# The combine of two expert outputs on one core: 16 rows of zeroes, 4096 bytes long in place of 512, taken from the last load room

## The chip, the cores and the metric

The kernel runs on one core of one Trainium2 chip. The metric is device time in microseconds, the median of several executions. VectorE (DVE) and ScalarE (ACT) compute; SyncE (SP) and ACT issue DMAs, each on a queue of its own. In the profile q1 is SP's queue and q10 is ACT's. Both are served by the same 16 DMA engines of the core.

## The reference

```python
def reference(expert_outputs, combine_weights):     # (16, 1024, 2, 512), (16, 1024, 2), float32
    weights = combine_weights[..., np.newaxis]
    return np.sum(expert_outputs * weights, axis=2).astype(np.float32)   # (16, 1024, 512)
```

For each of 16 x 1024 = 16384 tokens two rows of 512 floats are multiplied by one weight each and added. The inputs are 67 MB of rows and 0.13 MB of weights, the output is 33.5 MB. There is little arithmetic to a byte.

## The kernel before, in words

The tokens are laid over 128 partitions, 128 tokens to a partition. Of these the first 115 (`main`) are consecutive tokens of the partition; the last 13 come from the end of the array. One token is 4096 bytes of input (two rows) in a partition.

The tokens of a partition are cut into ten tiles of 13 or 12 (`TILES`). The large SBUF tile `et` holds 51 tokens for each partition and is divided into four rooms (`ROOM`, with their starts in `SITE`); tile g goes to room g modulo 4. So four tiles can be in SBUF at a time, and the load of tile g + 4 has to wait until the store of tile g has read its result out of the room.

The work is ordered by hand. SP issues the loads (L76) one after the other: five at the start, of which the first brings only 2 tokens and the second the other 11 of tile 0, then tiles 1, 2 and 3 (the fifth load fills the last room). Each later load follows the store that frees its room. For most tiles (`WHOLE`) VectorE multiplies the whole room by the weights in place (L88) and adds the two halves (L97); the sum lies in the first half of the room, and the store (L130) writes it out from there. Tile 8 (`MIXED`) is shared with ACT (L92, L94, L96), and the last tile is done token by token by ACT (L102) and VectorE (L103). The stores go out on ACT's queue, except the last two, which SP issues: tiles 7 and 8 in one, and tile 9.

What the change touches stands ahead of the loop. VectorE sets a small tile `zt` to zero (L108). ACT then issues, in this order on its queue: a DMA that writes these zeroes into 16 places of the output (L111), the weights of the first 115 tokens (L79, called in L112), and the weights of the last 13 in two halves (L114). After that ACT loads its table and does a warm-up activation (L115). The 16 places are the starts of 16 equal stretches of 920 output rows. Eight partitions' output makes one such stretch. The zeroes are overwritten later by store 0, the store of tile 0, which therefore has to wait for them. The first product of VectorE (L88) needs the weights and the first two loads.

Of the kernel before, what the change touches and what calls it, by code (L numbers as in the profile page):

```python
# [1 line left out]

# [4 lines left out]


@with_exitstack
def kernel(  # L10
    ctx: ExitStack,
    tc: tile.TileContext,
    expert_outputs: bass.AP,
    combine_weights: bass.AP,
    out: bass.AP,
):

    nc = tc.nc
    b, s, k, h = expert_outputs.shape
    assert k == 2
    n = b * s
    P = nc.NUM_PARTITIONS
    per = n // P
    assert per * P == n

    ROOM = [13, 13, 12, 13]
    ROOMS = len(ROOM)  # L30
    SITE = [sum(ROOM[:i]) for i in range(ROOMS)]
    TILES = [13, 13, 12, 13, 13, 13, 12, 13, 13, 13]
    FIRST = [2, 11, 13, 12, 13]
    STORES = [[0], [1], [2], [3], [4], [5], [6], [7, 8], [9]]
    WHOLE = [0, 1, 2, 3, 4, 5, 6, 7]
    MIXED = [8]
    ALONE = 3
    FREE = {9: 0}
    LAST = 13
    assert all(c <= ROOM[g % ROOMS] for g, c in enumerate(TILES))  # L40
    assert sum(TILES) == per and [g for st in STORES for g in st] == list(range(len(TILES)))
    main = per - LAST
    starts = [sum(TILES[:g]) for g in range(len(TILES))]

    def rows(x):

        first = x[0 : P * main, :].rearrange("(p t) f -> p t f", p=P)
        second = x[P * main : n, :].rearrange("(p t) f -> p t f", p=P)
        return lambda t, c: first[:, t : t + c, :] if t < main else second[:, t - main : t - main + c, :]

    flat = out.rearrange("b s h -> (b s) h")
    eo = rows(expert_outputs.rearrange("b s k h -> (b s) (k h)"))
    cw = rows(combine_weights.rearrange("b s k -> (b s) k"))
    o = rows(flat)

    dt = mybir.dt.float32
    mult = mybir.AluOpType.mult
    add = mybir.AluOpType.add
    copy = mybir.ActivationFunctionType.Copy

    pool = ctx.enter_context(tc.tile_pool(name="all", bufs=1))
    et = pool.tile([P, sum(ROOM), k * h], dt)
    halves = et.rearrange("p j (k h) -> p (j k) h", k=k)
    wt = pool.tile([P, per * k], dt)
    wk = wt.rearrange("p (t k) -> p t k", k=k)
    zt = pool.tile([16, 128], dt)
    warm = pool.tile([P, 1], dt)

    def place(t):
        g = max(g for g in range(len(TILES)) if starts[g] <= t)  # L70
        return SITE[g % ROOMS] + t - starts[g]

    def load(t, c, **kw):
        at = place(t)
        assert place(t + c - 1) == at + c - 1
        nc.sync.dma_start(out=et[:, at : at + c], in_=eo(t, c), **kw)  # L76

    def weights(q, t, c):
        q.dma_start(out=wk[:, t : t + c, :], in_=cw(t, c))  # L79

    def combine(g, base):
        at, c, t0 = SITE[g % ROOMS], TILES[g], starts[g]
        if g in WHOLE or g in MIXED:
            room = halves[:, k * at : k * (at + c), :]
            x0, x1 = et[:, at : at + c, 0:h], et[:, at : at + c, h : 2 * h]
            if g in WHOLE:
                wb = wt[:, k * t0 : k * (t0 + c)].unsqueeze(2).to_broadcast([P, k * c, h])
                nc.vector.tensor_tensor(out=room, in0=room, in1=wb, op=mult)  # L88
            else:
                for i in range(ALONE, c):  # L90
                    x = et[:, at + i, 0:h]
                    nc.scalar.activation(out=x, in_=x, func=copy, scale=wt[:, k * (t0 + i) : k * (t0 + i) + 1])  # L92
                w1 = wk[:, t0 : t0 + c, 1:2].to_broadcast([P, c, h])
                nc.vector.tensor_tensor(out=x1, in0=x1, in1=w1, op=mult)  # L94
                w0 = wk[:, t0 : t0 + ALONE, 0:1].to_broadcast([P, ALONE, h])
                nc.vector.tensor_tensor(out=x0[:, 0:ALONE], in0=x0[:, 0:ALONE], in1=w0, op=mult)  # L96
            nc.vector.tensor_tensor(out=halves[:, base : base + c, :], in0=x0, in1=x1, op=add)  # L97
            return
        for i in range(c):
            t = k * (t0 + i)  # L100
            x0, x1 = halves[:, k * (at + i), :], halves[:, k * (at + i) + 1, :]
            nc.scalar.activation(out=x0, in_=x0, func=copy, scale=wt[:, t : t + 1])  # L102
            nc.vector.scalar_tensor_tensor(  # L103
                out=halves[:, base + i, :], in0=x1, scalar=wt[:, t + 1 : t + 2], in1=x0, op0=mult, op1=add
            )

    with tc.manual_schedule():
        nc.vector.memset(zt, 0.0)  # L108

        ahead = flat[0 : P * main, :].rearrange("(q t) h -> q (t h)", q=16)  # L110
        nc.scalar.dma_start(out=ahead[:, 0:128], in_=zt)  # L111
        weights(nc.scalar, 0, main)  # L112
        for half in (slice(0, P // 2), slice(P // 2, P)):
            nc.scalar.dma_start(out=wk[half, main:per, :], in_=cw(main, per - main)[half])  # L114
        nc.scalar.activation(out=warm, in_=nc.const_aps.tensor(1.0, (P, 1), dt), func=copy)  # L115

        t = 0
        for i, c in enumerate(FIRST):
            load(t, c, **({"max_dma_last_dim": k * h * 4} if i == 0 else {}))
            t += c  # L120
        assert t == sum(TILES[:ROOMS])
        for j, st in enumerate(STORES):
            room = FREE.get(st[0], st[0] % ROOMS)
            base, c = SITE[room] * k, 0
            for g in st:
                combine(g, base + c)
                c += TILES[g]
            assert c <= k * ROOM[room]
            q = nc.sync if j in (7, 8) else nc.scalar
            q.dma_start(out=o(starts[st[0]], c), in_=halves[:, base : base + c, :])  # L130
            for g in st:
                if g + ROOMS < len(TILES):
                    load(starts[g + ROOMS], TILES[g + ROOMS])


# [1 line left out]
_INS = ['expert_outputs', 'combine_weights']  # L137
_OUTS = [((16, 1024, 512), 'float32')]


# [23 lines left out]
```

## Time and profile before

| what | value |
|---|---|
| median of 3 runs | 238.86 us (238.84 to 238.99) |
| span of the profiled execution, first to last instruction | 237.1 us |
| VectorE busy | 190.0 us, 80% of the span |
| ACT busy | 15.8 us, 7% |
| moved by DMA | 100.80 MB, mean 425 GB/s over the span |
| zeroes: memset, DMA | 165 ns; 8 KB, 3.9 us from issue to landing |
| weights of 115 tokens | 115 KB, 18.2 us from issue to landing |

The profiled execution's time is known by its span; the runs' median is 1.8 us above it, which is what lies around the first and the last instruction. "Busy" leaves out the instructions that only issue DMAs, wait or branch. The DMA row of the page shows the mean share of the 16 DMA engines' time in each of 40 slices, in tenths. The groups of instructions give the line, the engine, the tiles written and read, the shape, and how long one takes. In the chain of waits each row is a start, a duration and what was then being waited for.

### The profile page before, as it was taken

The numbers are of one execution on the slowest core, as the hardware profiler recorded it, in microseconds if no ns is written. First come the engines' busy times: TensorE is split into PE (matmuls) and PEld (weight loads), VectorE is DVE, ScalarE is ACT, GpSimd is POOL, SyncE is SP. The second block draws the span as 40 slices with busy tenths as digits, with TensorE's granted clock in tenths as the row PEclk, the third lists the DMA queues.
The fourth block names the chain that finished last, engine by engine and source line by source line (L and its number), as shares of the span: only waits on it lengthen the run. The fifth ranks groups of instructions, "written<-read, shape, count | busy, mean of one in ns | idle before, by whom it ended". The sixth has DMA issues, their size and how long they took to land.

```text
span 237.1 us, 154 instructions
## 1 busy us (share of the span) xinstructions
DVE 190.0 (80%) x33; ACT 15.8 (7%) x25; POOL 0.2 (0%) x4
## 2 busy tenths in 40 slices
DVE  0006999999999999999999998998499969919400
ACT  2000000000000000000000000000000055019200
POOL 0000000000000000000000000000000000000000
DMA  8999999989999999999899999999899999899996
GB/s 300 388 481 434 432 421 398 470 348 485 449 431 458 431 440 390 486 420 420 359 492 409 409 509 392 431 503 431 359 431 503 420 397 483 381 431 431 431 431 287
DMA packets 3344, 100.80 MB, mean 425 GB/s; under 512 B 512, under 2 KB 656, under 8 KB 912
## 3 DMA queue, kind: packets, MB, share of 16 engines
q1 hardware_dynamic: 2000, 77.33, 75.9%
q10 hardware_dynamic: 1344, 23.47, 23.0%
HBM read 67.24 MB, written 33.56 MB: 425 GB/s over the span
## 4 chain that ended last, share of the span: by engine, by line
DVE 55%; DMA 36%; issue 1%; ACT 0%; DVEq 0%; ACTq 0%; SPq 0%
DVE et L88 35%; DVE et L97 17%; DMA out_dram<-et 17%; DMA et<-in_expert_outputs_dram 12%; DMA wt<-in_combine_weights_dram 8%; DVE et L103 3%; ACT et L102 0%; DVEq L159 0%; ACTq L111 0%; DVE zt L108 0%; DVEq L88 0%; SPq L76 0%; ACTq L102 0%
## 5 line engine op out<-in xcount | busy, mean ns | idle before, releaser
L88 DVE TENSOR_TENSOR et<-et,wt 128x13312 f32<-128x13312 f32 (+1 forms) x8 | 110.0, 13754 | 23.8 <-DMA wt<-in_combine_weights_dram 18.7
L97 DVE TENSOR_TENSOR et<-et 128x6656 f32<-128x6656 f32 (+1 forms) x9 | 62.8, 6973 | 0.4
L92 ACT ACTIVATE et<-et,wt 128x512 f32<-128x512 f32 x10 | 6.2, 708 | 188.0 <-DMA et<-in_expert_outputs_dram 188.0
L103 DVE SCALAR_TENSOR_TENSOR et<-et,wt 128x512 f32<-128x512 f32 x13 | 8.7, 747 | 5.0 <-ACT et L102 5.0
L102 ACT ACTIVATE et<-et,wt 128x512 f32<-128x512 f32 x13 | 8.1, 707 | 14.0 <-DMA et<-in_expert_outputs_dram 14.0
L94 DVE TENSOR_TENSOR et<-et,wt 128x6656 f32<-128x6656 f32 x1 | 7.1, 7093 | 2.3 <-DMA et<-in_expert_outputs_dram 2.3
L96 DVE TENSOR_TENSOR et<-et,wt 128x1536 f32<-128x1536 f32 x1 | 1.8, 1751 | 0.0
L115 ACT ACT_TABLE_LOAD x1 | 1.3, 1283 | 3.1 <-issue 3.1
L108 DVE MEMSET zt<- 16x128 f32 x1 | 0.2, 165 | 0.8 <-PEq L148 0.8
L115 ACT ACTIVATE warm<-const-float32-1.0 128x1 f32<-128x1 f32 x1 | 0.2, 203 | 0.0
L148 POOL MEMSET const-bfloat16-1.0<- 128x1 bf16 x1 | 0.1, 102 | 0.0
L148 POOL MEMSET const-uint8-127<- 128x1 uint8 x1 | 0.1, 101 | 0.0
L148 POOL MEMSET const-float32-0.0<- 128x1 f32 x1 | 0.1, 99 | 0.2 <-issue 0.2
L148 POOL MEMSET const-float32-1.0<- 128x1 f32 x1 | 0.1, 98 | 0.0
## 6 DMA issues: line engine op xcount, KB each, us to landing
et<-in_expert_outputs_dram SPq DMA_DIRECT2D x7, 6656.0 KB, 32.2
out_dram<-et ACTq DMA_DIRECT2D x5, 3328.0 KB, 34.7
et<-in_expert_outputs_dram SPq DMA_DIRECT2D x2, 6144.0 KB, 41.1
out_dram<-et SPq DMA_DIRECT2D x1, 6656.0 KB, 19.9
out_dram<-et ACTq DMA_DIRECT2D x2, 3072.0 KB, 37.2
et<-in_expert_outputs_dram SPq DMA_DIRECT2D x1, 5632.0 KB, 18.2
out_dram<-et SPq DMA_DIRECT2D x1, 3328.0 KB, 14.0
et<-in_expert_outputs_dram SPq DMA_DIRECT2D x1, 1024.0 KB, 5.0
```

Of the source, the lines that this page charges most:

```text
L88: nc.vector.tensor_tensor(out=room, in0=room, in1=wb, op=mult)
L92: nc.scalar.activation(out=x, in_=x, func=copy, scale=wt[:, k * (t0 + i) : k * (t0 + i) + 1])
L94: nc.vector.tensor_tensor(out=x1, in0=x1, in1=w1, op=mult)
L96: nc.vector.tensor_tensor(out=x0[:, 0:ALONE], in0=x0[:, 0:ALONE], in1=w0, op=mult)
L97: nc.vector.tensor_tensor(out=halves[:, base : base + c, :], in0=x0, in1=x1, op=add)
L102: nc.scalar.activation(out=x0, in_=x0, func=copy, scale=wt[:, t : t + 1])
L103: nc.vector.scalar_tensor_tensor(out=halves[:, base + i, :], in0=x1, scalar=wt[:, t + 1 : t + 2], in1=x0, op0=mult, op1=add)
L108: nc.vector.memset(zt, 0.0)
L115: nc.scalar.activation(out=warm, in_=nc.const_aps.tensor(1.0, (P, 1), dt), func=copy)
L148: nc = _bacc.Bacc("TRN2", target_bir_lowering=False, num_devices=1)
```

## The change

The tile `zt` of 16 x 128 floats is no longer allocated. In its place a view of `et` is taken: partitions 0 to 15, the first token of the last room, all 1024 floats of it. It is set to zero by the same memset, now of 16 x 1024 elements. The DMA writes 1024 floats (`k * h`), two output rows, at each of the 16 places, in place of 128 floats, a quarter of a row. The room is filled by the fifth load afterwards, so this load has to come after the zeroes have been read.

```diff
     wk = wt.rearrange("p (t k) -> p t k", k=k)
-    zt = pool.tile([16, 128], dt)
     warm = pool.tile([P, 1], dt)
...
     with tc.manual_schedule():
+        zt = et[0:16, SITE[ROOMS - 1], :]
         nc.vector.memset(zt, 0.0)
 
         ahead = flat[0 : P * main, :].rearrange("(q t) h -> q (t h)", q=16)
-        nc.scalar.dma_start(out=ahead[:, 0:128], in_=zt)
+        nc.scalar.dma_start(out=ahead[:, 0 : k * h], in_=zt)
         weights(nc.scalar, 0, main)
```

## The prediction

> **What bounds the kernel now.** I read the page first: its slices, the DMA queues and the share that the packets took.
>
> ```profile
> span 237.1 us, 154 instructions
> ...
> DVE 190.0 (80%) x33; ACT 15.8 (7%) x25; POOL 0.2 (0%) x4
> ...
> DMA  8999999989999999999899999999899999899996
> ...
> q1 hardware_dynamic: 2000, 77.33, 75.9%
> q10 hardware_dynamic: 1344, 23.47, 23.0%
> ```
>
> The two queues (q1 is issued by SP, q10 by ACT) fill 75.9% + 23.0% = 98.9% of what 16 DMA engines could do in the span. VectorE has 80%. Next, the busy time by stretches; the last two columns are the DMA share and GB/s.
>
> ```profile
> 1.80:5.00 3.20, 0.00 (x0) 1.49 (x2) 0.00 (x0) 1.00 0.99 315
> 8.30:10.00 1.70, 0.00 (x0) 0.00 (x0) 0.00 (x0) 1.00 1.00 433
> 41.60:49.50 7.90, 7.90 (x1) 0.00 (x0) 0.00 (x0) 1.00 0.99 406
> 1.80:236.00 234.20, 189.85 (x32) 15.79 (x25) 0.00 (x0) 1.00 1.00 430
> ```
>
> From 1.8 us to 236 us the DMA engines have no gap (share 1.00, 430 GB/s). So the time is the bytes over this rate, plus 1.8 us ahead of the first packet and 1.1 us behind the last. Two stretches run below the undisturbed 433 GB/s: the first 3.2 us (315) and the 7.9 us in which the first store starts (406).
>
> Then the chain of waits, which reads differently at first sight:
>
> ```profile
> 0.81 0.17 DVE zt L108
> ...
> 1.01 0.39 ACTq L111
> ...
> 1.43 18.21 DMA wt<-in_combine_weights_dram
> ...
> 19.73 14.04 DVE et L88
> ...
> 144.62 39.25 DMA out_dram<-et
> ...
> 183.92 28.80 DMA et<-in_expert_outputs_dram
> ...
> 213.56 8.04 DVE et L103 x12
> ```
>
> It begins with just what is changed: the memset of the zeroes, the issue of their DMA, the weights behind it, and at 19.73 the first product. That is a chain of starts. Whether a delay of it reaches the end is told by the waits of VectorE further on (in brackets the idle time before the row):
>
> ```profile
> 145.69 12.96 DVE L88 TENSOR_TENSOR et<-et,wt 128x12288 f32<-128x12288 f32 x1 [1.10 <-DMA et<-in_expert_outputs_dram]
> ...
> 169.18 14.03 DVE L88 TENSOR_TENSOR et<-et,wt 128x13312 f32<-128x13312 f32 x1 [3.94 <-DMA et<-in_expert_outputs_dram]
> ...
> 192.63 7.09 DVE L94 TENSOR_TENSOR et<-et,wt 128x6656 f32<-128x6656 f32 x1 [2.30 <-DMA et<-in_expert_outputs_dram]
> ...
> 208.61 14.02 SPq L130 DMA_DIRECT2D out_dram<-et  x2
> 212.80 8.07 ACT L102 ACTIVATE et<-et,wt 128x512 f32<-128x512 f32 x13 [13.95 <-DMA et<-in_expert_outputs_dram]
> 213.56 8.71 DVE L103 SCALAR_TENSOR_TENSOR et<-et,wt 128x512 f32<-128x512 f32 x13 [4.97 <-ACT et L102]
> ```
>
> VectorE waits for loads 1.10 + 3.94 + 2.30 + 4.97 = 12.3 us in the second half: a late start is caught up there, as long as the loads themselves do not come later.
>
> **The change part by part.** *The memset* grows from 16x128 to 16x1024. Its 0.17 us stands above; what an element costs on VectorE I take from two sizes of large instructions:
>
> ```profile
> L88 DVE TENSOR_TENSOR et<-et,wt 128x13312 f32<-128x13312 f32 x6 | 84.1, 14020 | 22.7 <-DMA wt<-in_combine_weights_dram 18.7 <-DMA et<-in_expert_outputs_dram 3.9
> L97 DVE TENSOR_TENSOR et<-et 128x6656 f32<-128x6656 f32 x7 | 49.6, 7092 | 0.3
> ```
>
> (14020 - 7092) / (13312 - 6656) = 1.04 ns. 896 more elements are 0.93 us; the memset takes 1.10 us. It is another operation, so the bounds are 0 (no growth) and 0.93; I take 0.93, the rate of the same engine. VectorE has nothing else to do before 19.73 us, so the engine itself loses nothing; what is late is the ACT queue behind it.
>
> *The ACT queue.* The zeroes are issued at 1.94 in place of 1.01, the weights at 2.36 in place of 1.43, and the last two slices of weights and the warm-up 0.93 us later too. ACT's own next work is far off, at L92, and it waits for a load. So only the landing of the weights counts.
>
> *The zeroes' transfer* is 16 packets of 4096 in place of 512 bytes, 57,344 bytes more. At 430 GB/s on DMA engines without a gap that is **0.13 us**; at the start's 315 GB/s it would be 0.18; the lower bound is 0, if it found a gap. I take 0.13, since its place, about 5 us, is where the slow start ends.
>
> *The weights' landing.* Here the packets of q10 in three looks count: 4.0 to 4.5 us, 6.6 to 8.3, 8.3 to 10.0, and then the issues with their size and time to landing.
>
> ```profile
> DMA packets 78, 0.20 MB, mean 410 GB/s; under 512 B 14, under 2 KB 30, under 8 KB 78
> ...
> DMA packets 32, 0.74 MB, mean 433 GB/s; under 512 B 0, under 2 KB 16, under 8 KB 16
> ...
> q10 hardware_dynamic: 16, 0.01, 2.5%
> ...
> et<-in_expert_outputs_dram SPq DMA_DIRECT2D x1, 6144.0 KB, 50.9
> wt<-in_combine_weights_dram ACTq DMA_DIRECT2D x1, 115.0 KB, 18.2
> out_dram<-zt ACTq DMA_DIRECT2D x1, 8.0 KB, 3.9
> ```
>
> In the first look the zeroes (16 packets of 512 bytes and 14 of their landing marks) pass between the small packets of the first load. In the second and third look, which read the same, each of the 16 engines gives q10 one small packet of weights in 1.7 us, beside one large packet of the second load. The weights' 128 packets are 8 turns of this kind per engine, 13.6 of their 18.2 us. So their landing moves by turns. If their first packet still makes the turn at 6.6 us, they land 0.13 us later; if it misses it, one turn later, and this turn is one of the third load: 6656 KB in 8 pieces are 852 KB, 1.97 us at 433 GB/s; if the zeroes miss the gap between the first two loads as well, two turns, 3.9 us. The first product starts between 19.9 and 23.7 us. I expect 19.9 or 21.8; no row tells how long before 6.6 us the weights were ready.
>
> The Trainium skill, page "DMA: Bandwidth & Descriptors", section "Queues, rings and completion order", has an engine drain a whole packet, 9 to 17 descriptors typically, from one queue before it turns to the next. By that rule the 8 pieces of an engine would pass in one turn, the weights would not hold the first product at all and being late would cost nothing. The trace disagrees: one piece in each 1.7 us.
>
> *What covers it.* Store 0 follows the first product and sum, and so is up to 3.9 us later. What it must not do is leave the DMA engines without work. The row of the fifth load (in a look from 4.9 to 5.0 us, which holds its issue), and the issue of the sixth, which waits for store 0:
>
> ```profile
> et<-in_expert_outputs_dram SPq DMA_DIRECT2D x1, 6656.0 KB, 71.7
> ...
> 67.80 23.95 SPq L76 DMA_DIRECT2D et<-in_expert_outputs_dram  x2
> ```
>
> The fifth load lands at 4.9 + 71.7 = 76.6, the sixth is issued at 67.8: q1 has 8.8 us of work in hand. A store piece is half as long as a load piece and they alternate, so 1 us of delay of store 0 takes some 1.5 us from this; 3.9 us take 5.9 and leave 2.9. q1 does not run dry, and if it did for a moment, q10 would still hold a store. So the DMA engines go on without a gap; loads come slightly earlier, stores later, and the last load, with all bytes before it, at the same time plus 0.13. If the cover were gone, the price would be the delay itself.
>
> *The room.* The zeroes now lie where the fifth load goes, so that load must wait until they are read. It already waits for them:
>
> ```profile
> SPq L76 <- DMA out_dram<-zt: 2.1, 1, 2.1
> ```
>
> The zeroes land at 1.0 + 3.9 = 4.9 us; the wait gets longer, to between 5.9 and some 9 us. Behind it on SP stands only the sixth load of 67.8 us; and q1 needs the fifth only when the fourth is done, the 6144 KB that took 50.9 us from their issue and so landed past 50.9 us. Cost 0. Store 0, which overwrites the zeroed rows, comes 30 us after they land: 0. The tile that goes away frees 512 bytes: 0.
>
> **Sum.** 237.1 + 0.13 = 237.3 us of span. The median of the runs is 238.86, 1.8 us over the span, and nothing of the change lies there: 238.86 + 0.13 = **239.0 us**. What a measurement can tell from no change is about 0.2%, 0.48 us; this is less.
>
> **The rivals.** *Slower, through the weights.* The chain of waits is right to its end: the first product 2.1 us late (one turn and the zeroes' bytes), the rest behind it, 238.86 + 2.1 = 241.0. For it: this chain, and VectorE's work without a wait from 19.7 to 145 us. Against it: the 12.3 us of waits after that, and a DMA share of 1.00. It decides if store 0 comes over 8.8 / 1.5 = 5.9 us late, three turns. Chance 0.09.
>
> *Slower, through a cold write path.* Larger zeroes meet reads in the start. A start of that sort has a price in the rows: 3.2 us at 315 in place of 433 GB/s are 0.87 us lost. If the zeroes bring as much again, 239.9. Against it: the 512-byte packets took no visible extra time in the first look (410 GB/s). Chance 0.10.
>
> *Faster, through the first store.* The stretch from 41.6 to 49.5 us loses 7.9 x (1 - 406/433) = 0.49 us when writing begins in earnest. If zeroes of two whole rows take that over, 238.86 + 0.13 - 0.49 = 238.5; only with part of the start's 0.87 it is under the 0.2%. Against it: 64 KB are little beside a store of 3328 KB, and places in the output touched before are touched now. Chance 0.10, of which 0.05 are beyond 0.2%.
>
> *The change does not do what it says*: the rows could be cut into 512-byte packets, 8 on each engine. Packets of that size went through between others in the first look, so the time stays 239.0; it is within the main case.
>
> **How the numbers follow.** Main case, and its variant with more turns: 0.71, at 239.0, own range 238.8 to 239.2. Slower by over 0.2%: 0.09 + 0.10 = 0.19. Faster: 0.05. Same: 0.71 + 0.05 = 0.76. The range goes from 238.5 (the first store's loss gone) to 239.6 (most of a cold start's price); beyond are the first rival and the tail of the others, under 0.2.
>
> **What would show it.** Right: the memset near 1.1 us; the weights' landing moved by 0.1, 2.1 or 4 us and the first product with it; VectorE's waits after 145 us shorter by as much; DMA share 1.00 from 1.8 us to the end; the last load's landing and the span within 0.3 us of before. Wrong: a gap in the DMA share, a fall of the GB/s at about 5 us, or the stretch of the first store at another rate.

## The result and the profile after

The changed kernel takes 239.53 us (median of 7 runs, 239.44 to 241.43) against 238.90 us before: ratio 1.0038, 95% interval 1.0025 to 1.0050 (the ratios are worked out over all runs and are not the quotients of the two medians). It is slower by 0.6 us, outside what I had called no change, and inside the range of 238.5 to 239.6. One line of the source is gone ahead of the loop, so L88 is now L87, L97 is L96 and so on.

The profiled execution took 239.77 us, with a span of 238.0 us, 0.8 us over that of before. The chain of waits of the changed kernel (start, duration, what was waited for) begins:

```profile
0.99 0.92 DVE et L108
...
1.94 0.39 ACTq L111
...
2.36 21.19 DMA wt<-in_combine_weights_dram
...
23.64 14.04 DVE et L87
...
186.68 26.85 DMA et<-in_expert_outputs_dram
...
214.37 8.04 DVE et L102 x12
```

The memset takes 0.91 us, 0.75 more than before. The weights start 0.93 us later and land 3.9 us later. The first product comes at 23.64 in place of 19.73. But the last tile's work is only 0.8 us later. What lies between is seen in the timeline of the second half:

```profile
169.05 14.03 DVE L87 TENSOR_TENSOR et<-et,wt 128x13312 f32<-128x13312 f32 x1 [1.09 <-DMA et<-in_expert_outputs_dram]
...
192.52 7.09 DVE L93 TENSOR_TENSOR et<-et,wt 128x6656 f32<-128x6656 f32 x1 [2.33 <-DMA et<-in_expert_outputs_dram]
...
214.37 8.70 DVE L102 SCALAR_TENSOR_TENSOR et<-et,wt 128x512 f32<-128x512 f32 x13 [5.89 <-ACT et L101]
```

The wait of 1.10 us at 145 us is gone and that of 3.94 us is down to 1.09. So by 169 us VectorE has made up for its late start: its row there begins 0.13 us earlier than before. The loads are what comes late at the end. The DMA engines have no gap either; the row of the stretches (DMA share and GB/s last) reads as before:

```profile
1.80:236.00 234.20, 189.86 (x33) 15.79 (x25) 0.00 (x0) 1.00 1.00 431
```

A share of 1.00 does not say that the packets were as short as they can be. In both kernels the packets of the fourth load (12 tokens, 49152 bytes each) take 1.82 us. The packet that an engine has in hand just ahead of its first packet of store 0 takes longer. In a look at the DMA queues that holds the starts of just these 16 packets, one on each engine, the share times the length of the look is their mean duration. Before, from 41.6 to 43.4 us and from 43.4 to 45.7 us:

```profile
q1 hardware_dynamic: 16, 0.79, 101.2%
...
q1 hardware_dynamic: 16, 0.79, 95.8%
```

After, from 47.0 to 49.8 us, and behind it store 0's own first packets, from 49.8 to 50.8:

```profile
q1 hardware_dynamic: 16, 0.79, 97.5%
...
q10 hardware_dynamic: 16, 0.43, 98.7%
```

That is 1.012 x 1.8 = 1.82 us undisturbed, 0.958 x 2.3 = 2.20 us at the first store before, and 0.975 x 2.8 = 2.73 us after. The loss at the first store has grown from 0.38 to 0.91 us on each engine (a mean over the 16). Behind it the packets take their usual time in both kernels, so nothing wins this back. The starts of the packets in the trace give the whole account. The last packet of each engine is a mark of 4 bytes behind the last store. These marks come at 235.76 us on the mean of the engines before and at 236.33 after, 0.57 later. That is 0.53 for the first store and 0.13 for the longer zeroes, less 0.11, since the engines reach the second load at 5.19 before and at 5.08 after. The last mark of all comes at 235.97 before and at 236.82 after, 0.85 later, and it is the one that counts. So some 0.3 us of this span's 0.8 are unevenness: the engines end 0.3 us apart before and 0.8 after.

In what follows "the loss" is always this: how much longer than usual an engine holds the load packet that stands just ahead of its first packet of store 0.

### The profile page after: what moved, and what is told of

It reads as the page before. It is cut to its first block, busy times and chain, and to the rows that moved or that the text cites. A ratio compares the mean times of both kernels' runs of the same rounds, so it can differ in the third digit from the quotient of the medians.

```text
span 238.0 us, 155 instructions
## 1 busy us (share of the span) xinstructions
DVE 190.7 (80%) x33; ACT 15.8 (7%) x25; POOL 0.2 (0%) x4
## 4 chain that ended last, share of the span: by engine, by line
DVE 52%; DMA 36%; issue 5%; ACT 0%; DVEq 0%; ACTq 0%; SPq 0%
DVE et L87 35%; DMA out_dram<-et 16%; DVE et L96 13%; DMA et<-in_expert_outputs_dram 11%; DMA wt<-in_combine_weights_dram 9%; DVE et L102 3%; DVE et L108 0%; ACT et L101 0%; DVEq L159 0%; ACTq L111 0%; DVEq L87 0%; SPq L75 0%; ACTq L101 0%
## 5 line engine op out<-in xcount | busy, mean ns | idle before, releaser
L87 DVE TENSOR_TENSOR et<-et,wt 128x13312 f32<-128x13312 f32 (+1 forms) x8 | 110.0, 13753 | 22.8 <-DMA wt<-in_combine_weights_dram 21.7
L96 DVE TENSOR_TENSOR et<-et 128x6656 f32<-128x6656 f32 (+1 forms) x9 | 62.8, 6973 | 0.4
L108 DVE MEMSET et<- 16x1024 f32 x1 | 0.9, 912 | 1.0 <-PEq L148 1.0
```

## The experiments

Theory A: it is the late store 0 that costs, whatever made it late. Theory B: the longer zeroes cost by themselves. Theory C: their place in the room costs. The others are named where they came up.

### The parts of the change one by one

Short zeroes behind the long memset:

```diff
-        nc.scalar.dma_start(out=ahead[:, 0 : k * h], in_=zt)
+        nc.scalar.dma_start(out=ahead[:, 0:128], in_=zt[:, 0:128])
```

> The memset covers 16x1024 in the last room as in the changed kernel, but the DMA writes only the first 512 bytes of each row. Theory A (the late start: the longer memset makes the weights miss two turns, store 0 starts 3.9 us later, and the price of the first store's start grows with it): first product near 23.6 us, time 239.4 to 239.5, nearly all of the changed kernel's loss. Theory B (the bytes: longer zeroes cost their 0.13 us and something on the write path): first product late all the same, time 238.8 to 239.0.

239.40 us, ratio 1.0028 (1.0017 to 1.0039); first product at 23.45. This is 0.52 us of the loss with no byte added, as theory A has it. The changed kernel stands 0.13 us above it, and 0.22 in a second measurement below; that fits the forecast price of the bytes, but the runs of one kernel lie 0.1 us and more apart. From 47.0 to 49.6 us the profile has

```profile
q1 hardware_dynamic: 16, 0.79, 98.1%
```

0.981 x 2.6 = 2.55 us, a loss of 0.73 us.

Short zeroes and the short memset, in the room:

```diff
-        zt = et[0:16, SITE[ROOMS - 1], :]
+        zt = et[0:16, SITE[ROOMS - 1], 0:128]
...
-        nc.scalar.dma_start(out=ahead[:, 0 : k * h], in_=zt)
+        nc.scalar.dma_start(out=ahead[:, 0:128], in_=zt)
```

> Only the place of the zeroes is changed: 16x128 in the last room, 512 bytes a row, the short memset. Theories A and B both expect the kernel before: first product near 19.7 us, 238.9 us. Theory C (the place: reading the zeroes from the room, or the fifth load's order behind them, costs): 239.3 or more.

238.85 us against 238.88, ratio 1.0000 (0.9991 to 1.0009). The place costs nothing; theory C is out.

Long zeroes, the weights ahead of them:

```diff
-        nc.scalar.dma_start(out=ahead[:, 0 : k * h], in_=zt)
         weights(nc.scalar, 0, main)
+        nc.scalar.dma_start(out=ahead[:, 0 : k * h], in_=zt)
```

> The zeroes are 4096 bytes long and come from the last room, but ACT issues the weights ahead of them. Theory A: the weights are not late, first product at 19.5 to 19.8 us, time 238.9 to 239.1. Theory B: first product on time, but the loss stays, 239.4 to 239.6.

239.74 us, but its runs spread from 239.10 to 241.01. The first product was on time (20.02). The loss at the first store was that of the kernel before. The engines were uneven from the start: 47 of the 63 packets that start from 5.2 to 6.2 us are small ones (pieces of the first load, two of the zeroes, and marks), and the engines come to the second load up to 0.85 us apart (0.33 before). By its time this is what B expected and not A; but the time is not lost at the first store, and the order of the queue is another one, so it does not settle which of them is right.

Without zeroes (memset and DMA left out):

```diff
-        nc.vector.memset(zt, 0.0)
...
-        nc.scalar.dma_start(out=ahead[:, 0:128], in_=zt)
```

> No zeroes at all: the memset and their DMA are left out, the output is the same. Theory A: the zeroes cost next to nothing by themselves, weights slightly earlier, 238.7 to 238.9. Theory B: without any writes ahead the first store pays for the start of the write path in full: the stretch of the first store loses more than 0.49 us, 239.2 or more.

239.57 us, ratio 1.0036 (1.0023 to 1.0048). The kernel with the short zeroes is 0.7 us faster. This is theory B's line (239.2 or more) and not A's (238.7 to 238.9). The trace shows where the time goes. The held packet loses 0.37 us, as before; but on 13 engines the next load packet, behind the first one of store 0, loses 0.4 to 0.6 us more, which in the kernel before takes its usual time. And store 0 does not begin together on all engines: 12 begin by 45.93 us and one at 46.51, the other three at 48.3 to 48.6 us, after one more packet of the load. That this is the want of zeroes is not shown. With them left out the weights go ahead, and the engines come to the second load up to 0.81 us apart, as in the run above, which is slow too and has zeroes.

Long zeroes, set by two engines to be ready earlier:

```diff
-        nc.vector.memset(zt, 0.0)
+        nc.vector.memset(zt[:, 0 : k * h // 2], 0.0)
+        nc.gpsimd.memset(zt[:, k * h // 2 : k * h], 0.0)
```

> The changed kernel with its zeroes set by VectorE and GpSimd, one half each, so that the zeroes are ready some 0.5 us earlier and pass between the small packets of the first load. Theory A: weights and first product nearly on time (19.8 to 20.2 us), time 238.9 to 239.1, only the 0.13 us of the bytes. Theory B (the longer zeroes cost by themselves): 239.4 or more with the first product on time. If the first product still comes at 21.7 or later, it tells nothing between them.

239.67 us; the first product came at 23.42, so the zeroes missed the gap again, and it tells nothing between A and B.

### Store 0 late without a change to the zeroes

In the kernel before, memsets of a spare tile are put between the first product and its sum. They move store 0 and nothing ahead of it (N is 2, 4, 7, 10, 15, 22 or 30):

```diff
                 nc.vector.tensor_tensor(out=room, in0=room, in1=wb, op=mult)
+                for _ in range(N if g == 0 else 0):
+                    nc.vector.memset(pad, 0.0)
```

The first four were made for a theory P: that store 0 becomes ready a fixed time after its issue.

> The kernel before, with 2 memsets of 128x128 on VectorE between the first product and its sum; store 0 is issued some 0.3 us later and nothing else changes. Theory P (phase: store 0's first packet comes a fixed 4.9 to 5.3 us after the issue, and each DMA engine holds the read that it is on until then; so the loss is this time less the moment at which the read would have ended by itself): the loss at the first store grows by the delay, from 0.43 to some 0.75 us an engine, time 239.2. Theory A (lateness: each us of delay costs a little, 0.5 us for 3.9): 238.9.

> The same with 4 memsets, some 0.65 us. Theory P: near the edge; the loss is about 1.1 us (239.5) if the engines still wait for the store at the end of the same read, or near 0 (238.4 to 238.6) if they go on to another read first. Theory A: 239.0.

> The same with 7 memsets, some 1.1 us. Theory P: past the edge, the store is ready before the next read ends, no loss at the first store: 238.4 to 238.6, faster than the kernel before. Theory A: 239.0.

> The same with 10 memsets, some 1.6 us, nearly one read (1.8 us) later. Theory P: the loss comes back toward that of the kernel before, 0 to 0.3 us an engine, 238.5 to 238.8. Theory A: 239.1.

> The kernel before with 15 memsets of 128x128 between the first product and its sum: zeroes and weights stay as they are, but store 0 is issued some 3.5 us later, about as late as in the changed kernel. Theory A (the late store 0 is what costs, whatever made it late): the loss at the first store 0.7 to 0.9 us an engine, 239.4 to 239.5. Theory D (not the lateness but something at the start, the zeroes and weights that meet the large reads of the second load): 238.9 to 239.1.

| N | store 0 issued at | time, us | runs | ratio (95% interval) |
|---|---|---|---|---|
| 0 (before) | 40.9 | 238.87 | 238.80 to 240.53 | |
| 2 | 41.0 | 238.88 | 238.79 to 240.91 | 1.0007 (0.9992 to 1.0021) |
| 4 | 41.3 | 239.73 | 238.88 to 239.91 | 1.0030 (1.0019 to 1.0042) |
| 7 | 42.1 | 239.18 | 239.07 to 239.36 | 1.0007 (0.9996 to 1.0019) |
| 10 | 43.0 | 239.75 | 238.84 to 240.52 | 1.0029 (1.0017 to 1.0042) |
| 15 | 44.3 | 239.63 | 239.49 to 239.68 | 1.0030 (1.0019 to 1.0042) |

Theory P falls: with 7 memsets the loss was not near 0 but 0.5 us as with none, and store 0's first packets began at 47.5 us with 7 and with 10 memsets, though the issues lie 0.9 us apart. What moves is the packet of the load behind which the store comes, not the time after the issue.

With 2 memsets the loss was 0.69 us (from 43.2 to 45.8 us the 16 packets take 96.6% of 2.6 us), nearly that of late512, and the median time was that of before; so the loss alone does not give the time. The end of the next section takes this up.

With 4 and 10 memsets the runs fall into two groups, near 238.9 and from 239.6 up. The profiles are of the upper group, and there one engine goes on to another packet of the load while the other 15 begin the store. With 10 memsets, the last marks from 235.6 to 236.0 and from 236.0 to 236.9 us:

```profile
DMA packets 15, 0.03 MB, mean 67 GB/s; under 512 B 14, under 2 KB 14, under 8 KB 14
...
DMA packets 1, 0.00 MB, mean 0 GB/s; under 512 B 1, under 2 KB 1, under 8 KB 1
```

One engine ends alone, at 236.7 us (the fifteenth packet of the first look, the only large one, is its last piece of the store). The core waits for this one.

With 15 memsets, zeroes and weights as before and store 0 as late as in the changed kernel, the whole loss is there. From 46.7 to 49.9 us:

```profile
q1 hardware_dynamic: 16, 0.79, 100.0%
```

3.20 us, a loss of 1.38, more than the 0.7 to 0.9 that theory A expected. So the late store 0 is enough to bring the loss about, and theory D, which blamed what happens at the start, falls. But 7 and 10 memsets, 1.2 and 2.1 us, had not raised the loss on most engines, which a price per microsecond of lateness does not explain.

Both kernels were run once more as they are:

> The kernel before once more, for a second profile of it: the loss at the first store again 0.4 to 0.5 us an engine, 238.9.

> The changed kernel once more, for a second profile: first product near 23.6 us again (the zeroes miss the gap between the first two loads), the loss at the first store 0.7 to 1.0 us an engine, 239.5.

238.86 and 239.62 us; both losses came out above what was expected. The second profile of the kernel before has a loss of 0.61 us at the first store, more than the 0.38 of the first one, and the same end: its first reads went better, as the stretch of 1.8 to 3.4 us shows (first profile, then second).

```profile
1.80:3.40 1.60, 0.00 (x0) 0.31 (x1) 0.00 (x0) 1.00 0.95 210
...
1.80:3.40 1.60, 0.00 (x0) 0.25 (x1) 0.00 (x0) 1.00 1.02 292
```

The second profile of the changed kernel has a loss of 1.22 us with first reads as good as this (305 GB/s). Compared like with like, the change adds 0.5 to 0.6 us at the first store in both pairs. In this second profile the engines end 0.3 us apart, as in the kernel before, and its span is 237.8 us against 237.2. So the unevenness need not come with the change.

### The border between two loads

In the changed kernel, and with 15 memsets, the packet that is held is the eighth and last of the fourth load. In the kernel before it is the sixth of the eight. Theory E: the loss is larger where the first store meets the border between two loads. Theory W: the zeroes do something for the first store that wears off.

> The kernel before with 22 memsets ahead of the sum, store 0 some 5.4 us late, so that its first packets come behind the first piece of the fifth load, not at the border between the fourth and the fifth. Theory E (the border: the loss is larger only where the first store meets the end of a load): loss at start and first store together back at 1.1 us an engine, 238.9 to 239.1. Theory A (lateness): 1.7 us or more, 239.6 or more.

> The same with 30 memsets, some 7.5 us late, one piece further. Theory E: 238.9 to 239.1. Theory A: 239.6 or more, growing.

Past the border the loss is small again. The border by itself costs nothing either: in the kernel before the engines come to the last packet of the fourth load at 49.6 to 49.9 us, with store 0 under way, and it takes the usual 1.82 us. With 22 memsets, from 48.5 to 51.1 us, and with 30, from 50.5 to 53.1 us (first and second packet of the fifth load, usual length 1.97 us):

```profile
q1 hardware_dynamic: 32, 0.85, 92.6%
```

```profile
q1 hardware_dynamic: 16, 0.85, 91.1%
```

2.41 - 1.97 = 0.44 and 2.37 - 1.97 = 0.40 us, as in the kernel before. So lateness as such is not the price at the first store. The times were 240.69 (1.0060 to 1.0084) and 240.48 us (1.0058 to 1.0089), far from theory E's 238.9 to 239.1 and within theory A's "239.6 or more". What speaks against A is where the time is lost, which is later in the kernel. Now q1 does run dry. With 22 memsets, from 72.6 to 78.0 us:

```profile
q10 hardware_dynamic: 108, 2.45, 108.4%
q1 hardware_dynamic: 16, 0.00, 0.2%
...
et<-in_expert_outputs_dram SPq DMA_DIRECT2D x1, 6656.0 KB, 30.0
```

q1 has nothing but the marks of the fifth load; the sixth, issued in this stretch at 73.6 us, begins at 78.0. Around its return the engines lose 1.3 us each on the mean in a few packets, 1.1 with 30 memsets, though q10 had work all the time.

Zeroes written again, shortly before store 0, in the kernel before and in that with 15 memsets:

```diff
                 nc.vector.tensor_tensor(out=room, in0=room, in1=wb, op=mult)
+                if g == 0:
+                    nc.vector.memset(zt, 0.0)
+                    nc.scalar.dma_start(out=ahead[:, 0:128], in_=zt)
```

> The kernel before, but the 512-byte zeroes are written a second time after the first product, some 8 us ahead of store 0. Theory W (the zeroes open the output's rows for the first store, and this wears off by the time it comes): loss at the first store smaller than 0.4 us an engine, 238.4 to 238.7. Theory E and A: 238.9.

> The same second writing in the kernel with 15 memsets, some 14 us ahead of its late store 0. Theory W: back at 238.9. Theories E and A: 239.6 as without it.

239.09 (1.0005 to 1.0022) and 239.77 us: no gain in either. In the first one store 0 is issued at 42.17, 1.3 us later than before, so the run with 7 memsets (issued at 42.14, 239.18 us) is its match; its loss is 0.60 against 0.49 there. In the second one the loss is 1.13, still that of the border. Theory W expected a gain from writing the zeroes again, and there is none.

At last a border was put under a store 0 that is on time, by cutting the fourth load 9 and 3, and for control 6 and 6:

```diff
-    FIRST = [2, 11, 13, 12, 13]
+    FIRST = [2, 11, 13, 9, 3, 13]
```

> The kernel before, store 0 on time, but the fourth load is cut in two, 9 and 3 tokens, so that a border between two loads falls at about 45.5 us, where the first packets of store 0 come. Theory E (the border): the loss at the first store rises from 0.4 to 0.6 us an engine to 1.1 or more, 239.4 to 239.7. Theory A (lateness): 238.9, since store 0 is not late.

> The control: the same load cut 6 and 6, the borders at about 41.8 and 49.1 us, away from the first packets of store 0. Both theories: 238.8 to 239.0. If it is slow as well, the smaller pieces cost by themselves and border9 tells nothing.

239.60 (1.0027 to 1.0054) and 239.24 us (1.0007 to 1.0024). With 9 and 3, the packets from 43.7 to 46.2 us, the last ones of the first piece, ahead of store 0:

```profile
q1 hardware_dynamic: 16, 0.59, 101.2%
```

2.53 us where such a packet otherwise takes 1.37 (16 of them from 41.0 to 42.3 us, 105.1%): a loss of 1.16 us, with the first product at 19.48 and store 0 issued at 40.67. This is theory E's number. But the control did not come out at 238.9: cutting the load costs 0.36 us by itself. What was written ahead of the control says that border9 then tells nothing by its time. What is left is the difference between the two cuts, 0.36 us of time, and the loss of 1.16 us.

Over all profiles the border shows more clearly when the start is counted too. A better start goes with a larger loss: in the kernel before the engines reach the second load at 5.19 us with a loss of 0.38 in the first profile, and at 4.93 with 0.61 in the second. So the two are best added. Ten profiles have uncut loads, the weights behind the zeroes, and store 0 away from the border on at least 15 engines: before (twice), room512, rezero, and 2, 4, 7, 10, 22 and 30 memsets. There the sum of the mean start of the second load and the loss is 5.35 to 5.65 us. In the six with store 0 at the border (after twice, late512, split4096, rezero15 and 15 memsets) it is 5.86 to 6.25. The loss alone is 0.26 to 0.69 us in the ten and 0.73 to 1.38 in the six.

## Why the prediction was wrong

**The bytes: right.** 0.13 us were forecast. The trace shows them directly: a zero packet of 4096 bytes takes 0.159 us (19.9% of 0.8 us in the look below), one of 512 bytes in the kernel before 0.027. By the runs the changed kernel stands 0.13 or 0.22 us above the one with short zeroes and nearly the same lateness.

**The memset: a little off.** 0.75 us more, not 0.93. The zeroes missed the gap all the same.

**The weights' turns: the mechanism right, my pick wrong.** I gave 19.9 to 23.7 us for the first product and expected 19.9 or 21.8. It was 23.64, two turns: the zeroes came a little after the small packets of the first load had ended. From 6.3 to 7.1 us q10 has the 16 zeroes, from 8.2 to 8.9 us their 16 marks, and only from 9.8 us the first weights:

```profile
q10 hardware_dynamic: 16, 0.07, 19.9%
...
q10 hardware_dynamic: 16, 0.00, 1.3%
```

**The room and the fifth load: right.** The zeroes landed at 9.2 us and the fifth load was issued behind them; this cost nothing, and the place alone costs nothing.

**What covers it: half right, and here the prediction failed.** VectorE did catch up, and q1 kept 2.9 us of work in hand, as I had worked out (the fifth load landed at 75.3, the sixth was issued at 72.4). But I concluded that with no gap on the DMA engines a late store 0 costs nothing, and the sum has no term for it. I had seen the slow stretch of the first store (0.49 us) and used it only as something that could be won. I did not ask whether moving the store would make it dearer. It did: the store came behind the last packet of the fourth load, and the loss on each engine rose from 0.38 to 0.91 us, and from 0.61 to 1.22 in the second pair of profiles. That the DMA share stayed at 1.00 was right, and it did not mean what I took it to mean. That the time still fell into the range of 238.5 to 239.6 is luck: its upper end came from a cold start's price, which was not paid.

**"If it did for a moment, q10 would still hold a store": wrong too**, in a case that the change does not reach. With 22 and 30 memsets q1 ran dry beside a full q10, and the engines lost 1.3 and 1.1 us on its return.

**The rivals.** "Slower, through the weights" had the right start and the right sign, but not the way: it would have brought the whole delay to the end, and of 3.9 us only some 0.5 came there. I let it decide only from 5.9 us of delay. "Slower, through a cold write path" was for the longer zeroes; no packet shows them to cost more than their bytes. "Faster, through the first store" did not come: with long zeroes and store 0 on time (wfirst4096) the loss was 0.45 us, no smaller than before. The rows were not cut into packets of 512 bytes: q10 had 16 packets of 0.07 MB together. I had put 0.19 on slower together and 0.76 on the same.

**How an engine changes queues.** The Trainium skill ("DMA: Bandwidth & Descriptors", "Queues, rings and completion order") has an engine drain a whole packet of several descriptors before it changes queues (such a packet is a group of pieces; what the profile counts as a packet is here one piece). The trace of the changed kernel disagrees as that of before did: zeroes, marks and first weights each wait for one packet of the second load.

**What stays open.** Why the loss is larger at the border is not shown. That it goes with the border rests on the six profiles with the store there (0.73 to 1.38 us) against the ten with the store elsewhere (0.26 to 0.69), above all on 22 and 30 memsets, which are later still; the load cut 9 and 3 adds little weight, since its control is slow too. Why the six differ so much among themselves is open. Whether the run without zeroes is slow for want of them or because the weights go earlier is open too.

## What to carry to other kernels

A DMA share of 1.00 over a whole span says that there is no gap, not that nothing can be lost: look at how long the same packet takes at different places, above all where a queue begins to work or comes back from idle. If small transfers share engines with large ones, ask in which gap between the large packets they pass now and by how much they may slip, since here each miss cost a turn of a large packet, 1.7 to 2.0 us. And where all engines are full, the slowest of the 16 sets the end, so an event that one engine meets differently shows in the time.

## What the runs showed of the hardware that was not expected

- In the first profile of the kernel before the start read at 210 GB/s and the loss at the first store was 0.38 us; in the second 292 GB/s and 0.61 us. The ends agree within 0.1 us. The better start was given back at the first store, which began at 45.9 us on the mean in both.
- The kernel without the 8 KB of zeroes at the start took 239.57 us against 238.88 with them, and lost more at the first store, though this moves 3328 KB. The weights go earlier then, and which of the two costs is not shown. Writing the zeroes again later brings nothing (239.09 us).
- When q1 came back after some 7 us without data to move, the engines lost 1.3 us each (22 memsets) and 1.1 us (30 memsets), though q10 kept them full in between.
- With 7 memsets, and with the zeroes written twice, the span was that of before (237.1 us) but the same execution took 239.19 and 239.14 us, 2.0 us over it in place of 1.8. What lies outside the span was not looked into.
